# Reordering the first projection of a two-branch encoder block: transposes, bank reads, operand splits and gate outputs

## The chip, the core and the metric

The kernel runs on one core of one Trainium2 chip. The time of a kernel is the device time of one execution in microseconds (us); for each kernel the median of several runs is given. The engines named below are PE (matrix multiply, with its weight loads PEld), DVE (vector), ACT (scalar and activation), POOL (GpSimd) and SP, which here only issues DMAs.

## The reference

One layer (DEPTH is 1) of a block over a sequence of 2048 rows of 1024 float32 values:

```
xn = rmsnorm(x, norm1_g)
z = xn @ w_in                       # [pool | q | f | i | o | branch gates]
gates = sigmoid(zg + b_gate)
ya = pool_mixer(u_pool, ...) @ w_pa
yb = hgrn2_mixer(zq, zf, zi, zo, ...) @ w_pb
x = x + (gates[0] * ya + gates[1] * yb) @ w_o
x = x + conv_glu_ffn(rmsnorm(x, norm2_g), w_up, conv_w, conv_b, w_down)
return rmsnorm(x, final_g)
```

The pooling mixer takes means over windows of 2, 4, 8 and 16 rows. The HGRN2 mixer is a gated linear recurrence with 4 heads of 128; its value input is zi and its output is multiplied by silu(zo). The feed-forward part has 2816 hidden channels for value and gate, with a causal convolution of width 3.

## The kernel before

**Tiling.** The 2048 rows are worked on in two rounds of 1024 rows. A round holds two blocks of 512 rows, b and b+1. Each round runs the input projections, the two mixers, the output projection and the feed-forward part. Weights come in from memory as raw tiles of 128 x 512.

**Seven products.** Every large matrix product splits the rows, the contraction and the columns into halves, and forms the 2 x 2 block product with seven multiplications, called P1 to P7, in place of eight. Each of the seven multiplies one combination of x blocks with one combination of weight blocks. The combinations of x (table FORM) are B11 for P1, B21 for P2, T2 for P6, T1 for P5, T3 for P7, T4 for P4 and B22 for P3. With x12 and x22 the two halves of block b+1, T1 is x12 - B11, T2 is x22 - T1, T3 is B11 - T2, T4 is B21 - T2 and B22 is -x22. Each has four tiles, k = 0 to 3.

**Split operands.** Every operand is split into a high and a low part in the type fp32r: ACT casts the high part, then DVE subtracts it from the source for the low part (function split, lines 615 and 616, for x; Stream.convert, lines 212 and 213, for weights). A product takes three matmuls (high x high, high x low, low x high).

**The first projection.** Function proj_io, line 1187 on, makes zi ("v") and zo ("z") for 1024 rows. It is the first large product of a round. It runs the passes in the order P1, P2, P6, P5, P7, P4, P3. One pass has four weights (k) times four groups of 128 rows (j) times three matmuls, 48 in all. The results stand in PSUM in four tiles per letter: P1 in X, P2 in Y, P6 and P7 and P4 accumulate in Z, P5 and P3 accumulate in V. PSUM has eight such tiles (pool "banks" with bufs=8), so a letter needs four of them and must wait until others have been read. The readers are: e1, a copy of X by ACT (L1210); v, which reads Y after P2 (L1064); u2, which reads Z after P6 (L1214); u3, which reads Z after P7 (L1216) and must have done so before P4 adds to the same Z; z of block b+1, which is u3 + V and must have read V before P3 adds to it; z of block b, which reads Z after P4 (L1063). Both z go through SiLU on ACT and out by a DMA on SP.

**Where the x forms come from.** forms_a_task transposes block b on PE for B11 and B21. forms_b_task does the same for block b+1: turned(k) transposes one 128-column group (four transposes of 128 x 128, L678) into one PSUM tile, and turned(k) and turned(k + 4) together serve T1 and T2 of number k (L766, DVE). T3 and T4 are subtractions of tiles in SBUF (L796 and L804, DVE).

**Weights of this projection.** The weights have numbers in the stream: w0 to w3 for P1, w4 to w7 for P2, w8 to w11 for P6, w12 to w15 for P5, w16 to w19 for P7, w20 to w23 for P4 and w24 to w27 for P3. Those of P6 take two additions on DVE, those of P7 and P3 one (L352); all take the split. Intermediate sums are kept in memory by DMAs on SP and loaded again for P5 and P3.

**What sets the order.** The functions emit instructions in Python order. Tasks (generators) are stepped between matmuls: every six matmuls make a tick, which advances the weight stream by one and steps each task that is due. A planner then orders each engine's instructions by emission and by its own simulation of when each is ready, so the order on the chip is not the emission order. On the chip each engine works its list in order. behind(a, b) forces a after b on one engine without a semaphore; stream.pins does so for a weight's split. In proj_io the first matmul of each k of P2 from k = 1 is put behind the last transpose made so far, the four T4 and B22 tiles are split in turns, and u3 is followed at once by z of block b+1.

Of the kernel before, what the change touches and what calls it, by code (L numbers as in the profile page):

```python
# [15 lines left out]
ALU = mybir.AluOpType  # L16
# [14 lines left out]
NT = TB // P  # L31
# [21 lines left out]
FIRST = ("P1", "P6", "P5")  # L53
# [27 lines left out]
def tile_trunk(  # L81
# [16 lines left out]
    pe, act, dve, pool, sp = nc.tensor, nc.scalar, nc.vector, nc.gpsimd, nc.sync  # L98
# [9 lines left out]
    def slot(name, cols=TB, dt=F32):  # L108
        return slots.tile([P, cols], dt, tag="s", name=name, padded_shape=[P, 528])

    def bank(name, cols=512):
        return banks.tile([P, cols], F32, tag="b", name=name, padded_shape=[P, 512])

    def f32(ap):
        return ap.bitcast(F32)
# [30 lines left out]
    def mm(*args, **kw):  # L146
        count[1] = pe.matmul(*args, **kw)  # L147
        count[0] += 1
        if count[0] % MM_PER_TICK == 0:
            tick()  # L150
# [89 lines left out]
    def behind(ins, other):  # L240

        tc.add_manual_dep(ins.ins, other.ins.name, mybir.DependencyInfo(
            mybir.DependencyClass.NoSync, mybir.DependencyReason.DATA), reason="behind")
# [17 lines left out]
    stream = Stream()  # L261
# [285 lines left out]
    def col(o):  # L547
        return cols[:, o : o + 1]
# [57 lines left out]
    setup = []  # L606


    def split(src, name, on_pool=False):
        hi = slot(name + "h", TB, F32R)  # L610
        lo = slot(name + "l", TB, F32R)
        if on_pool:
            pool.tensor_scalar(hi, src, 1.0, 0.0, ALU.mult, ALU.add)
        else:
            act.copy(hi, src)
        dve.tensor_tensor(lo, src, f32(hi), ALU.subtract)  # L616
        return hi, lo

    def chain_t(ps, w_of, xs, start=True, stop=True):
# [8 lines left out]
    def n_step(ps, w, xk, j, first, last, mark=None, **kw):  # L628
        xh, xl = xk
        a, b = xh[:, j * P : (j + 1) * P], xl[:, j * P : (j + 1) * P]  # L630
        mm(ps, a, w[:, 0], start=first, stop=False, **kw)
        if mark is not None:
            behind(count[1], mark)
        mm(ps, a, w[:, 1], start=False, stop=False, **kw)
        mm(ps, b, w[:, 0], start=False, stop=last, **kw)
# [40 lines left out]
    def transpose(ps, xs, j, k):  # L676
        c = (k % 4) * P
        return pe.transpose(ps[:, j * P : (j + 1) * P], xs[j, k // 4][:, c : c + P], ident)  # L678
# [68 lines left out]
    def forms_b_task(src, gain, forms, full, after, go, early):  # L747
        name = f"{src[0]}{src[1]}_"
        xs = {}
        while early and not forms["B21"]:  # L750
            yield 1
        yield from norm_rows(src, name, xs, after, int(early))
        while not go():
            yield 2
        t1, b12, b22 = [], [], []

        def turned(k):
            ps = bank(f"{name}t{k}")
            for j in range(NT):
                forms["turned"] = transpose(ps, xs, j, k)  # L760
            return ps

        def minus(key, k, ps, x1, c=None, op=ALU.subtract):
            t = slot(f"{name}{key}{k}")
            c = gain + (k if c is None else c)
            dve.scalar_tensor_tensor(t, ps, col(c), x1, ALU.mult, op)  # L766
            return t


        t3 = []  # L770
        for k in range(4):
            while len(full["B11"]) <= k:
                yield 4
            p12 = turned(k)
            p22 = turned(k + 4)
            t = slot(f"{name}b{k}")
            act.activation(t, p22, AF.Copy, scale=negs[:, gain + k + 4 : gain + k + 5])
            b22.append(t)
            t1.append(minus("t1", k, p12, full["B11"][k]))
            t2 = minus("t2", k, p22, t1[k], k + 4)  # L780
            if src[0] == "m":
                t = slot(f"{name}t3{k}")
                pool.tensor_tensor(t, full["B11"][k], t2, ALU.subtract)
                t3.append(t)
            elif not early:
                t3.append(minus("t3", k, p12, b22[k], op=ALU.add))
            forms["T2"].append(split(t2, f"{name}T2{k}"))
            full["T2"].append(t2)
            yield 1
        for k in range(4):  # L790
            forms["T1"].append(split(t1[k], f"{name}T1{k}"))
            yield 5
        for k in range(4):
            if early:
                t = slot(f"{name}t3{k}")
                dve.tensor_tensor(t, full["B11"][k], full["T2"][k], ALU.subtract)  # L796
                t3.append(t)
            forms["T3"].append(split(t3[k], f"{name}T3{k}"))
            yield 1
        for k in range(4):  # L800
            while len(full["B21"]) <= k:
                yield 4
            t4 = slot(f"{name}t4{k}")
            (dve if src[0] == "x" else pool).tensor_tensor(t4, full["B21"][k], full["T2"][k],  # L804
                                                           ALU.subtract)
            forms["T4"].append(split(t4, f"{name}T4{k}"))
            forms["B22"].append(split(b22[k], f"{name}B22{k}"))
            yield 1

# [377 lines left out]
    def proj_io(b0, forms, late, vd, zd):  # L1187
        bk = {}
        e1, u2, u3 = {}, {}, {}

        def temp(d, key, j):
            d[j] = slot(f"io{b0}_{key}_{j}")
            return d[j]

        def out_v(hf, j, a):
            t = slot(f"v{b0}_{hf}_{j}")
            ins = value(t, a, bk["Y" if hf == 0 else "V"][j])
            if not (b0 or hf):
                behind(ins, stream.low)
            sp.dma_start(vd[hf][:, j, :], t)  # L1200

        def out_z(hf, j, a):
            t = slot(f"z{b0}_{hf}_{j}")
            value(t, a, bk["Z" if hf == 0 else "V"][j])
            act.activation(t, t, AF.Silu)
            sp.dma_start(zd[hf][:, j, :], t)

        def after(p, j):
            if p == "P1":
                act.copy(temp(e1, "e1", j), bk["X"][j])  # L1210
            elif p == "P2":
                out_v(0, j, (e1[j], "add"))
            elif p == "P6":
                dve.tensor_tensor(temp(u2, "u2", j), e1[j], bk["Z"][j], ALU.subtract)  # L1214
            elif p == "P7":
                dve.tensor_tensor(temp(u3, "u3", j), bk["Z"][j], e1[j], ALU.subtract)  # L1216
                out_z(1, j, (u3[j], "add"))
            elif p == "P4":
                out_z(0, j, (e1[j], "from"))
            elif p == "P3":  # L1220
                out_v(1, j, (u2[j], "sub"))

        for p in IO_ORDER:
            if p == "P7" and not b0:
                setup.append(Task(setup_task()))
            xs = need(forms, FORM[p], late)
            kb = "Y" if p == "P2" else BANK[p]
            if kb not in bk:
                bk[kb] = [bank(f"io{b0}_{kb}_{j}") for j in range(NT)]
            for k in range(4):  # L1230
                if (p, k) == GO_IO[b0 > 0]:
                    go_io[0] = True
                mark = None
                if p == "P2" and k and not b0:
                    while len(forms["T2"]) < k:
                        late.step()
                    mark = forms["turned"]
                    while len(stream.tiles) < 9 + k:
                        stream.convert()
                w = stream.get("io")  # L1240
                if (p, k, b0) == ("P1", 0, 0):
                    xh, xl = xs[0]
                    for n in range(3):
                        for j in range(NT):
                            mm(bk[kb][j], (xl if n == 2 else xh)[:, j * P : (j + 1) * P],
                               w[:, n % 2], start=n == 0, stop=False, skip_group_check=True)
                    stream.used(1)
                    continue
                for j in range(NT):
                    n_step(bk[kb][j], w, xs[k], j, p in FIRST + ("P2",) and k == 0, k == 3, mark,  # L1250
                           skip_group_check=True)
                    mark = None
                    if k == 3:
                        after(p, j)
                stream.used(1)
# [453 lines left out]
    for b in range(0, SEQ // TB, 2):  # L1709
        forms, task, late = nxt  # L1710
        if b:
            join(task)
        forms, task, late = mixer(b, forms, late)
# [52 lines left out]
```

## Time and profile before

| | us |
|---|---|
| median of 3 runs | 2564.29 |
| lowest and highest run | 2561.81, 2565.13 |
| the profiled execution | 2561.69 |
| its span, first to last instruction | 2560.0 |
| PE busy | 2516.1 (98%) |
| DVE busy | 1979.3 (77%) |
| ACT busy | 1177.7 (46%) |
| POOL busy | 749.1 (29%) |

In the views of the trace, a row of the waits reads "engine, tile, line <- engine, tile, line that it waited for: total us, times, longest". A row of the windows gives, for a stretch of the span, each engine's busy time with its number of instructions, then the clock granted to PE as a share of the full one, the busy share of the DMA engines, and GB/s. A row of the timeline gives start, duration, engine, line, operation, output <- inputs, number of instructions merged, and in brackets the idle time of the engine before it and what ended that.

### The profile page before, as it was taken

Reading aid. Unit: us, or ns where it says so; the run is one execution under the profiler, and the core shown is the slowest. Engines: PE = TensorE matmul, PEld = TensorE weight load, DVE = VectorE, ACT = ScalarE, POOL = GpSimd, SP = SyncE. Lnnn points to the kernel's source line nnn. Section 1 sums busy time; section 2 is a strip of 40 time slices with the busy share of each in tenths; the row PEclk is TensorE's granted clock in tenths of the full one; section 3 lists DMA queues with packets and bytes.
Section 4 is the critical chain, followed back from the end, with each engine's and each line's share of the span. In section 5 each row is a group of like instructions: output and inputs, shape, how many; then the busy total and the mean of one; then the engine's idle time right before and its main releaser. Section 6 shows DMA issues by size and latency. Waiting matters only on the chain.

```text
span 2560.0 us, 35657 instructions
## 1 busy us (share of the span) xinstructions
PE 2516.1 (98%) x11508; PEld 2055.6 (80%) x11508; DVE 1979.3 (77%) x3518; ACT 1177.7 (46%) x2218; POOL 749.1 (29%) x1117
## 2 busy tenths in 40 slices
PE   8899999999999999999999999999999999999998
PEld 7688877888788888888887888888887888888887
DVE  7798879588889787885585777675978987778755
ACT  5434433424645454554454344442355554545534
POOL 1244344001544334461230111200034433334410
PEclk9999999999999999999999999999999999999999
DMA  6777768768788878997344343446442454446952
GB/s 235 247 191 210 225 181 244 240 206 244 196 241 247 220 230 239 257 356 261 129 153 149 94 134 118 128 150 229 144 165 94 153 152 144 145 139 229 333 162 99
DMA packets 252332, 493.76 MB, mean 193 GB/s; under 512 B 26544, under 2 KB 43056, under 8 KB 251824
## 3 DMA queue, kind: packets, MB, share of 16 engines
q1 hardware_dynamic: 185664, 315.70, 38.2%
q0 software_dynamic: 41504, 110.64, 16.8%
q10 hardware_dynamic: 24976, 65.13, 7.3%
q8 instruction: 91, 1.49, 0.2%
q14 instruction: 97, 0.79, 0.1%
HBM read 381.79 MB, written 187.17 MB: 222 GB/s over the span
## 4 chain that ended last, share of the span: by engine, by line
PE 71%; DVE 1%; ACT 1%; issue 0%; POOL 0%; POOLq 0%; DVEq 0%; ACTq 0%
PE dn_P L147 16%; PE up_Z L147 14%; PE up_V L147 9%; PE up_X L147 9%; PE wo_P L147 3%; PE gr_Z L147 3%; PE gr_X L147 2%; PE gr_V L147 2%; PE pb L147 2%; PE pa L147 2%; PE fr_Z L147 1%; PE io_Z L147 1%; PE io_V L147 1%; PE fr_X L147 1%; PE fr_V L147 1%; PE pl L931 1%
## 5 line engine op out<-in xcount | busy, mean ns | idle before, releaser
L212 ACT CAST ops<-raw 128x512 fp32r<-128x512 f32 x736 | 454.5, 620 | 839.3 <-PE dn_P L147 175.6
L213 DVE TENSOR_TENSOR ops<-raw,ops 128x512 fp32r<-128x512 f32 x736 | 547.9, 748 | 210.0 <-ACT ops L212 204.7
L1502 DVE SCALAR_TENSOR_TENSOR e<-h,cols,e 128x512 f32<-128x512 f32 x176 | 143.6, 818 | 30.8 <-ACT e L1500 24.0
L1500 ACT ACTIVATE e<-h,cols 128x512 f32<-128x512 f32 x176 | 142.6, 814 | 24.8 <-DVE h L1064 18.4
L1505 DVE SCALAR_TENSOR_TENSOR e<-h,cols,e 128x512 f32<-128x512 f32 x176 | 133.8, 769 | 2.8
L866 POOL DMA_DIRECT2D g_P<-dg_P x154 | 84.4, 555 | 161.9 <-PE dn_P L147 113.2
L1171 POOL TENSOR_TENSOR gf_P<-e,e 128x512 f32<-128x512 f32 x44 | 60.8, 1384 | 149.5 <-DVE e L1511 96.0
L1297 POOL TENSOR_TENSOR q<-q,qs 128x512 f32<-128x512 f32 x16 | 21.9, 1366 | 201.5 <-ACT qs L1296 194.4
L1171 POOL TENSOR_TENSOR gf_P<-gf_P,e 128x512 f32<-128x512 f32 x44 | 59.2, 1345 | 71.9 <-DVE e L1511 71.4
L1495 POOL COPY h<-h 128x2 f32<-128x2 f32 x88 | 40.4, 471 | 113.9 <-DVE h L1063 107.0
L1509 ACT ACTIVATE e<-e 128x512 f32<-128x512 f32 x88 | 55.5, 631 | 38.5 <-DVE e L1505 38.2
L1497 POOL COPY hist<-h 128x2 f32<-128x2 f32 x88 | 35.8, 407 | 118.2 <-DVE h L1064 116.4
L1064 DVE TENSOR_TENSOR h<-up_u,up_V 128x512 f32<-128x512 f32 x88 | 60.1, 683 | 13.3 <-PE up_V L147 12.8
L1334 ACT ACTIVATE gt<-gt,cols 128x512 f32<-128x512 f32 x48 | 34.8, 725 | 73.9 <-DVE gt L1064 55.0
L1146 DVE TENSOR_TENSOR x<-x,wo_P 128x512 f32<-128x512 f32 x88 | 55.9, 678 | 12.2 <-PE wo_P L147 12.0
L1146 DVE TENSOR_TENSOR ac<-ac,dn_P 128x512 f32<-128x512 f32 x72 | 47.0, 680 | 16.6 <-PE dn_P L147 16.4
L1525 POOL DMA_DIRECT2D dg_P<-gf_P x88 | 50.6, 575 | 7.9 <-POOL gf_P L1171 7.2
L1098 ACT COPY up_e<-up_X 128x512 f32<-128x512 f32 x44 | 25.8, 587 | 58.0 <-PE up_X L147 50.7
L916 POOL COPY qm<-q 128x64 f32<-128x64 f32 x64 | 21.1, 347 | 105.1 <-DVE q L922 36.9
L931 PE MATMUL pl<-qm,k 128*128 128x192 f32 x256 | 50.3, 326 | 0.3 <-DVE qm L920 0.3
L1495 POOL COPY h<-hist 128x2 f32<-128x2 f32 x88 | 46.3, 534 | 7.7 <-DVE m_T42l L616 7.7
L931 PEld LDWEIGHTS pl<-qm,k 128*128 128x128 f32 x256 | 44.2, 189 | 5.0 <-issue 0.6
(1301 smaller groups left out, 8107.4 us busy)
## 6 DMA issues: line engine op xcount, KB each, us to landing
g_P<-dg_P POOLq DMA_DIRECT2D x154, 256.0 KB, 6.0
raw<-in_w_up_t SPq DMA_DIRECT2D x132, 256.0 KB, 3.1
raw<-in_w_in_t SPq DMA_DIRECT2D x98, 256.0 KB, 3.3
dg_P<-gf_P POOLq DMA_DIRECT2D x88, 256.0 KB, 3.9
dg_P<-e SPq DMA_DIRECT2D x66, 256.0 KB, 3.3
raw<-in_w_dn SPq DMA_DIRECT2D x66, 256.0 KB, 3.6
x<-in_x SPq DMA_DIRECT2D x64, 256.0 KB, 5.1
gd<-gt ACTq DMA_DIRECT2D x64, 256.0 KB, 3.3
```

What stands on the lines that cost most here:

```text
L147: count[1] = pe.matmul(*args, **kw)
L212: self.mark = act.copy(hi, v)
L213: low = self.low = dve.tensor_tensor(lo, v, f32(hi), ALU.subtract)
L866: eng.dma_start(t, d)
L931: ins = pe.matmul(pa_[:, c * 192 : c * 192 + 192], ks[:, (i + c) * P : (i + c + 1) * P], mv[:, c].rearrange("p s x -> p (s x)"), start=Tru ...
L1064: return dve.tensor_tensor(dst, t, ps, ALU.add if how == "add" else ALU.subtract)
L1146: dve.tensor_tensor(t, t, ps[j], ALU.add if sg > 0 else ALU.subtract)
L1171: pin(eng.tensor_tensor(t, x0, x1, op))
L1495: pool.tensor_copy(h[:, 0:2], hist[:, mt] if hf == 0 else hs[s, 0][:, TB : TB + 2])
L1500: in_turn(act.activation(t, h[:, 2:], AF.Identity, bias=col(o_cb + mt), scale=col(o_cw + 4 * MF + mt)))
L1502: in_turn(second(dve.scalar_tensor_tensor(t, h[:, 1 : 1 + TB], col(o_cw + 2 * MF + mt), t, ALU.mult, ALU.add)))
L1505: dve.scalar_tensor_tensor(t, h[:, 0:TB], col(o_cw + mt), t, ALU.mult, ALU.add)
```

## The change

All of it concerns the first projection of the first round (the flag early, or b0 equal to 0); the second round keeps the old order.

1. Transposes for T2 in the second pass. Before P2's k = 1 the code now emits T1 and T2 of two numbers instead of one, before k = 2 of three, before k = 3 of all four. The list forms["turned"] holds the last transpose of every turned group. The matmuls of k = 1 for j = 2 and 3 are put behind the transposes of T2 number 0, all four j of k = 2 behind those of number 1, and all four j of k = 3 behind the first group of number 2. Before, only the j = 0 matmul of each k was bound. The weights w9 to w11 are emitted one k earlier.
2. Bank reads ahead of the last two T4 tiles. T4 numbers 2 and 3 are emitted only when all four u3 have been, and their subtraction is put behind the last u3 on DVE.
3. B22 behind T4. The four B22 splits are emitted after all four T4 splits, not in turns with them.
4. The gate behind T4. z of block b+1 (addition, SiLU, store) is emitted before k = 2 of P4, not right after each u3.
5. T4's weights behind T3. The split of w20 is put behind the split of T3's last tile on ACT and DVE.

```diff
+            up = act.copy(hi, src)
+        low = dve.tensor_tensor(lo, src, f32(hi), ALU.subtract)
+        last_split[0] = up, low
...
             for j in range(NT):
-                forms["turned"] = transpose(ps, xs, j, k)
+                ins = transpose(ps, xs, j, k)
+            forms.setdefault("turned", []).append(ins)
...
             forms["T3"].append(split(t3[k], f"{name}T3{k}"))
+            if early:
+                stream.pins[20] = last_split[0]
...
+            while early and k > 1 and len(forms.get("u3", ())) < 4:
+                yield 1
+            ins = (dve if src[0] == "x" else pool).tensor_tensor(t4, full["B21"][k],
+                                                                 full["T2"][k], ALU.subtract)
+            if early and k > 1:
+                behind(ins, forms["u3"][3])
             forms["T4"].append(split(t4, f"{name}T4{k}"))
+            if not early:
+                forms["B22"].append(split(b22[k], f"{name}B22{k}"))
+            yield 1
+        while len(forms["B22"]) < 4:
+            k = len(forms["B22"])
             forms["B22"].append(split(b22[k], f"{name}B22{k}"))
             yield 1
...
-                dve.tensor_tensor(temp(u3, "u3", j), bk["Z"][j], e1[j], ALU.subtract)
-                out_z(1, j, (u3[j], "add"))
+                ins = dve.tensor_tensor(temp(u3, "u3", j), bk["Z"][j], e1[j], ALU.subtract)
+                forms.setdefault("u3", []).append(ins)
+                if b0:
+                    out_z(1, j, (u3[j], "add"))
...
-                if p == "P2" and k and not b0:
-                    while len(forms["T2"]) < k:
-                        late.step()
-                    mark = forms["turned"]
-                    while len(stream.tiles) < 9 + k:
+                if p == "P2" and not b0:
+                    if k:
+                        while len(forms["T2"]) < min(k + 1, 4):
+                            late.step()
+                        mark = forms["turned"][k + (k > 1)]
+                    while len(stream.tiles) < min(10 + k, 12):
                         stream.convert()
+                if (p, k, b0) == ("P4", 2, 0):
+                    for j in range(NT):
+                        out_z(1, j, (u3[j], "add"))
...
-                    n_step(bk[kb][j], w, xs[k], j, p in FIRST + ("P2",) and k == 0, k == 3, mark,
-                           skip_group_check=True)
-                    mark = None
+                    n_step(bk[kb][j], w, xs[k], j, p in FIRST + ("P2",) and k == 0, k == 3,
+                           mark if k > 1 or j > 1 else None, skip_group_check=True)
```

No arithmetic instruction, transpose or DMA is added or removed; they change places.

More of the change, by code (lines that the diff above doesn't have):

```diff
@@ L606, in tile_trunk @@
     setup = []
+    last_split = [None]
     def split(src, name, on_pool=False):
@@ L612, in split @@
         if on_pool:
-            pool.tensor_scalar(hi, src, 1.0, 0.0, ALU.mult, ALU.add)
+            up = pool.tensor_scalar(hi, src, 1.0, 0.0, ALU.mult, ALU.add)
         else:
-            act.copy(hi, src)
-        dve.tensor_tensor(lo, src, f32(hi), ALU.subtract)
+            up = act.copy(hi, src)
+        low = dve.tensor_tensor(lo, src, f32(hi), ALU.subtract)
+        last_split[0] = up, low
         return hi, lo
@@ L803, in forms_b_task @@
             t4 = slot(f"{name}t4{k}")
-            (dve if src[0] == "x" else pool).tensor_tensor(t4, full["B21"][k], full["T2"][k],
-                                                           ALU.subtract)
-            forms["T4"].append(split(t4, f"{name}T4{k}"))
+            while early and k > 1 and len(forms.get("u3", ())) < 4:
[4 more added lines that the diff above has]
+                behind(ins, forms["u3"][3])
+            forms["T4"].append(split(t4, f"{name}T4{k}"))
+            if not early:
[3 more added lines that the diff above has]
+            k = len(forms["B22"])
             forms["B22"].append(split(b22[k], f"{name}B22{k}"))
```

## The prediction

> **What bounds the kernel now.** I read the page's totals first, then the list of PE's waits, then the windows of the passes that the change touches, and last the timelines of PE, DVE, ACT, POOL and SP inside them.
>
> ```profile
> span 2560.0 us, 35657 instructions
> ## 1 busy us (share of the span) xinstructions
> PE 2516.1 (98%) x11508; PEld 2055.6 (80%) x11508; DVE 1979.3 (77%) x3518; ACT 1177.7 (46%) x2218; POOL 749.1 (29%) x1117
> ```
>
> PE is busy in all but 43.9 us of the span (2560.0 - 2516.1). A reordering can win only those, and whatever PE spends at a reduced clock. PE's waits, longest first:
>
> ```profile
> PE io_Z L147 <- DVE io_u L1216: 8.4, 1, 8.4
> PE pl L971 <- DVE q L890: 5.2, 3, 2.3
> ...
> PE io_Z L147 <- DVE x_t L766: 1.9, 2, 1.1
> ...
> PE x_t L678 <- DVE x_t L766: 1.3, 2, 1.1
> ...
> PE io_Z L147 <- ACT x_T32h L615: 1.1, 1, 1.1
> ```
>
> Four of these rows (8.4, 1.9, 1.3 and 1.1) lie in the first projection. The passes follow, cut at PE's own starts: P2 with P6, P5, P7, the hole before P4, P4, P3.
>
> ```profile
> 27.50:57.35 29.85, 26.64 (x130) 21.09 (x129) 23.36 (x39) 13.67 (x27) 1.79 (x5) 1.00 0.46 151
> 57.35:68.45 11.10, 11.10 (x49) 8.83 (x48) 9.37 (x17) 3.93 (x7) 0.00 (x0) 1.00 0.98 324
> 68.45:81.43 12.98, 11.88 (x49) 8.79 (x48) 11.40 (x19) 5.61 (x10) 1.58 (x3) 1.00 0.80 269
> 81.43:89.83 8.40, 0.00 (x1) 0.04 (x1) 6.32 (x12) 3.41 (x6) 3.81 (x10) 0.64 0.00 0
> 89.83:102.91 13.08, 13.08 (x49) 10.55 (x49) 11.66 (x24) 7.98 (x12) 2.96 (x12) 0.84 0.66 205
> 102.91:114.02 11.11, 11.11 (x50) 9.01 (x49) 9.99 (x11) 3.65 (x6) 7.86 (x8) 1.00 0.80 294
> ```
>
> P5 and P3 show what an undisturbed pass takes, 11.1 us. Against that: P2 with P6 idles 29.85 - 26.64 = 3.2, P7 idles 12.98 - 11.88 = 1.1, the hole is 8.4, and P4 is 13.08 - 11.1 = 2.0 longer, at a granted clock of 0.84 after 0.64 in the hole. That makes 14.7 us, the most that the change can win inside these passes. DVE is busy in 72.1 of the 86.5 us, so it paces the stretch, and the change frees none of its time: it only sorts its list.
>
> **The change part by part.** One DVE operation on 128x512 costs 0.61 to 0.69 us in the rows below, which I use throughout.
>
> *T2's transposes (P2, P6).*
>
> ```profile
> 35.61 1.25 PE L678 MATMUL x_t<-ident,x_xs 128*128 128x128 f32 x10
> ...
> 48.98 0.73 PE L147 MATMUL io_Z<-ops,x_T20h 128*128 128x512 f32 x2 [1.12 <-DVE x_t L766]
> ```
>
> ```profile
> 30.97 0.88 DVE L672 TENSOR_SCALAR x_xs<-x,x_3r 128x512 f32<-128x512 f32 x2
> ...
> 36.68 0.75 DVE L766 SCALAR_TENSOR_TENSOR x_t<-x_t,cols,x_b 128x512 f32<-128x512 f32 x1 [2.79 <-PE x_t L678]
> ...
> 53.83 0.69 DVE L213 TENSOR_TENSOR ops<-w11s,ops 128x512 fp32r<-128x512 f32 x1 [0.74 <-ACT ops L212]
> ```
>
> The rows of x are scaled by 31.85 (30.97 + 0.88), but the transposes stand at 35.61 behind P2 matmuls in PE's list, while DVE idles 2.79 us for them. Later PE pays that back, waiting for T1/T2 to leave PSUM. With half of k = 1 and all of k = 2 bound behind the transposes, they can run at about 32, after the k = 0 products and two of k = 1. DVE then starts T1 some 4 us sooner, and w11's split (53.83) comes near 49.5. PE's own work allows 27.5 + 26.6 = 54.1 for the end of P6, with w11 wanted a k-pass of 2.8 us (11.1 / 4) before it, at 51.3. So DVE is no longer last. But letter Z still needs T2 number 3 off PSUM, so I leave 0.7 of the 3.2: **-2.5**. Bounds: -3.2, and +1.0 if the 32 transposes, now mandatory points in PE's list, catch a tile not yet free (the two such waits now are 1.3 together). DVE's additions for w9 to w11 move one k earlier; at worst one stands ahead of a T1, which is 0.6 us and inside the 0.7.
>
> *P5.* It starts sooner by the same amount. Its window shows DMA share 0.98, and w12 to w15 and T1 must come sooner too; they follow w11 on DVE and move with it. I cost this at nothing; if the loads don't move, the 2.5 is given back here.
>
> *T4's weights behind T3 (P7).*
>
> ```profile
> 74.11 1.89 DVE L213 TENSOR_TENSOR ops<-raw,ops 128x512 fp32r<-128x512 f32 x3
> 75.91 0.68 DVE L616 TENSOR_TENSOR x_T32l<-x_t,x_T32h 128x512 fp32r<-128x512 f32 x1
> ...
> 77.88 0.69 DVE L616 TENSOR_TENSOR x_T33l<-x_t,x_T33h 128x512 fp32r<-128x512 f32 x1
> 78.49 0.69 DVE L804 TENSOR_TENSOR x_t<-x_b,x_t 128x512 f32<-128x512 f32 x1
> ...
> 88.39 0.68 DVE L616 TENSOR_TENSOR x_B223l<-x_b,x_B223h 128x512 fp32r<-128x512 f32 x1
> 89.00 0.68 DVE L1216 TENSOR_TENSOR io_u<-io_Z,io_e 128x512 f32<-128x512 f32 x1
> ```
>
> Three splits for T4's weights (1.89 us, with three casts on ACT) stand ahead of T3 number 2, for which PE waits 1.1. Only w20 is pinned; w21 and w22 take later ops buffers and I take them to follow it. **-1.1**, between -1.1 and 0. Behind the pin on DVE's list stand w20's split and P4; the raw buffers that w20 to w23 release feed P3's weights, wanted some 11 us later, and a raw tile lands in 3.3 us, by the page's list of loads:
>
> ```profile
> raw<-in_w_in_t SPq DMA_DIRECT2D x98, 256.0 KB, 3.3
> ```
>
> *The hole.* Call P7's end E. The first u3 could read Z at about E - 2, but DVE has from 78.49 to 89.07 the whole T4 and B22 chain ahead of it: four subtractions and eight splits, 12 x 0.65 = 7.8, a mask cast, and four gaps of 0.68 in which ACT casts. Now only T4 numbers 0 and 1 come ahead. T3's last split ends at 78.57, E - 2.9; without the three weight splits (1.9) at about E - 4.2. From there DVE has the two subtractions, two T4 splits and two weight splits, 6 x 0.61 = 3.7, to E - 0.5, then the first u3 to E + 0.1. PE started 0.15 after it (89.68 to 89.83), and I allow one more operation ahead: P4 starts at **E + 0.7**, not E + 8.4, which is **-7.7**. Bounds: -8.4, and -4 if four more weight or B22 splits (2.5 us) and ACT gaps get ahead. T4 numbers 2 and 3 follow the last u3 (E + 2.6): two subtractions, an ACT cast, two splits, done by E + 5.8; P4 wants them 5.6 and 8.3 us after its start, so at E + 6.3 and E + 9.0.
>
> *The clock.* The only PE wait here with a reduced clock is the 8.4; the 1.1 in P7 has 1.00. With 0.7 left, P4 takes 11.1: **-2.0**, or 0 if some 4 us of wait stay. [...]
>
> *B22 and the gate behind T4 (P3).* What left the hole must now fit into P4's 11.1 us: three u3 and two T4 tiles (3 + 4 operations), two weight splits, four B22 splits, four z, two of P3's four weights (sum and split each): 7 + 2 + 4 + 4 + 4 = 21 operations, 21 x 0.61 = 12.8 us against the 11.8 from E to P4's end. The last z is not wanted at P3's first matmul but 2 us later, so a wait of **+0.5** (0 to +3). The other two weights (4 operations) are wanted 5.6 us into P3. The four z stores move behind P4 loads on SP; ACT's SiLUs and their table load move with them, and ACT has over 3 us free in each window. POOL's mask building is not moved.
>
> *Behind the projection.*
>
> ```profile
> 103.02 1.84 POOL L411 TENSOR_TENSOR w29s<-raw,raw 128x512 f32<-128x512 f32 x1 [5.87 <-DMA raw<-in_w_in_t]
> ```
>
> ```profile
> 116.80 0.39 PE L147 MATMUL fr_Z<-x_T20h,ops 128*128 128x512 f32 x1
> ```
>
> The next unit's summed weight waits for its raw tiles, which SP issues after P3's sums. Those sums come no later against P3 than now, so the 13.8 us from the sum to its use cover it. The planner lays out everything behind anew:
>
> ```profile
> 120.00:1400.00 1280.00, 1266.80 (x5795) 1034.38 (x5795) 1003.20 (x1729) 588.19 (x1109) 440.47 (x597) 1.00 0.75 222
> 1400.00:2560.00 1160.00, 1147.21 (x5246) 939.02 (x5244) 883.84 (x1635) 527.69 (x990) 280.20 (x444) 0.99 0.48 156
> ```
>
> PE idles 13.2 + 12.8 = 26.0 us there. I put **+0.5** on a new layout, between -2 and +3.
>
> The sum is -2.5 - 1.1 - 7.7 - 2.0 + 0.5 + 0.5 = **-12.3 us**. The profiled execution took 2561.69 (span 2560.0 and 1.69 around it), so 2549.4 by its own measure. It was the fastest execution shown, 2.6 below the median 2564.29; from the median the sum gives **2552.0 us**, my forecast.
>
> **The rivals.**
>
> *The hole shrinks, the rest doesn't.* DVE paces the stretch, and the two early parts only move its list. If the planner fills DVE's early gap with weight sums, P6 and P7 keep their 4.3, and if more than one split stays ahead of u3 the remainder is 3 and P3 waits 1. [...] For it speaks DVE's 72.1 of 86.5 us; against it the 2.79 that DVE spends waiting for PE's transposes.
>
> *It doesn't do what it says.* w21 and w22 get ahead of w20, and w20 to w23, three B22 splits and T4's casts still stand before u3 in DVE's list; the remainder is over 4 and the clock still falls: 4 from the hole, less 1 for P3, within the measurement: 2561.3. Against it: u3 is bound ahead of T4's subtractions by an explicit dependency, and B22 is emitted after them.
>
> *Slower: the layout behind it.* The level products of the recurrence (pl) sit in PE's list at places the planner chose, and three of them wait 5.2 us for q, 1.7 each. If the new layout puts them ahead of their q more often, each costs 1.7. The gain up to there, 12.8, is used up by 8 such waits (13.6), which is where this decides; 11 of them, 18.7, end at 2564.29 - 12.8 + 18.7 = 2570.2. For it: a few us of input timing change every later choice. Against it: only three among the rounds' many levels wait so now, and PE is at 99% in both windows.
>
> **How the numbers follow.** Runs here differ by 3.3 us (2561.81 to 2565.13); 0.2%, 5.1 us, is about what a measurement tells from no change. Chances: my forecast (a gain over 7) 0.57, the hole alone 0.18, no effect 0.10, slower through the layout 0.15. The hole alone counts as faster. So faster 0.75, same 0.11, slower 0.14 (part of the layout case ends within the bound). The best sum, all of 14.7 and 2 from the layout, would be 2547.6 from the median; runs near the lower end take another 1.5. The upper end takes in the hole alone with its worse bounds and a part of no effect: 2546 to 2562.5. The likeliest case alone spans 2547 to 2557.
>
> **What would show it.** After the change: the first T2 transposes near 32, DVE's wait of 2.79 gone, P6 ending near 54.6; no wait on T3; the row for io_Z on io_u under 2 us or gone, a granted clock of 1.00 through P4; P3 beginning by E + 12.5; the next unit's first matmul near 114.0 - 12.8 = 101.2. It is wrong if a wait over 4 us stands anywhere between 27 and 101, if DVE's T1 still starts after 35, or if PE's idle time past the projection grows by more than 3.

## The result and the profile after

| | before | changed |
|---|---|---|
| median, us (6 runs each) | 2565.09 | 2553.57 |
| lowest and highest | 2561.81, 2566.67 | 2551.22, 2555.53 |
| the profiled execution | 2561.69 | 2554.45 |
| its span | 2560.0 | 2552.7 |

The changed kernel takes 0.9956 of the time before, 95% interval 0.9943 to 0.9969: 11.5 us less by the medians. The prediction said 2552.0, 12.3 less. The two profiled executions lie 7.2 us apart, since that of before was the fastest of its six runs and that of after the second slowest.

Busy times hardly move: PE is busy for 2518.6 us in place of 2516.1, DVE for 1978.0 in place of 1979.3, ACT for 1176.0 in place of 1177.7.

The passes of the changed kernel, cut at the same places as before (P2 with P6, P5, P7, the hole, P4, P3; the columns are the stretch, its length, each engine's busy time and instructions, PE's granted clock, DMA share, GB/s):

```profile
27.08:52.92 25.84, 25.84 (x129) 21.42 (x128) 23.64 (x40) 14.62 (x29) 1.82 (x5) 1.00 0.55 180
52.92:63.98 11.06, 11.06 (x50) 9.02 (x48) 9.44 (x17) 2.86 (x5) 0.00 (x0) 1.00 0.96 320
63.98:75.22 11.24, 11.24 (x49) 8.83 (x47) 9.65 (x16) 4.99 (x9) 5.29 (x12) 1.00 0.66 227
75.22:78.31 3.09, 0.00 (x0) 0.03 (x1) 2.41 (x5) 0.62 (x1) 0.00 (x0) 0.85 0.83 266
78.31:92.20 13.89, 13.89 (x48) 11.18 (x49) 12.97 (x27) 7.76 (x13) 2.73 (x10) 0.79 0.39 127
92.20:104.45 12.25, 12.25 (x54) 9.94 (x53) 10.93 (x17) 6.33 (x12) 9.45 (x11) 1.00 0.99 329
```

P2 with P6 went from 29.85 to 25.84, P7 from 12.98 to 11.24, the hole from 8.40 to 3.09. P4 became longer, 13.08 to 13.89, at a clock of 0.79. P3 has 12.25 because the planner put four matmuls of the next unit into it (at 98.71 to 99.40; the count of 54 also takes in matmuls that cross the window's edges).

For comparing runs I use one number, "passes": from P2's first matmul to the end of P3's last, less 0.23 us for each of the next unit's matmuls in between. It is 86.5 before and 76.2 after, 10.2 less before rounding.

Five rows of DVE's timeline tell why a hole of 3.09 is left:

```profile
71.13 0.76 DVE L618 TENSOR_TENSOR x_T33l<-x_t,x_T33h 128x512 fp32r<-128x512 f32 x1 [0.74 <-ACT x_T33h L617]
71.81 0.72 DVE L812 TENSOR_TENSOR x_t<-x_b,x_t 128x512 f32<-128x512 f32 x1
72.46 2.53 DVE L213 TENSOR_TENSOR ops<-raw,ops 128x512 fp32r<-128x512 f32 x4
...
76.87 0.69 DVE L618 TENSOR_TENSOR x_T41l<-x_t,x_T41h 128x512 fp32r<-128x512 f32 x1 [0.68 <-ACT x_T41h L617]
77.48 2.48 DVE L1231 TENSOR_TENSOR io_u<-io_Z,io_e 128x512 f32<-128x512 f32 x4
```

All four weight splits of P4 (2.53 us) stand between T3's last split and u3, and T4 number 1 is subtracted only after T4 number 0's split, so that its cast on ACT leaves another gap of 0.68. The first u3 starts at 77.48, 2.3 us after P7's end.

### The profile page after: what moved, and what is told of

It is laid out like the page before. It is cut to its first block, busy times and chain, and to the rows that moved or that the text cites. A ratio compares the mean times of both kernels' runs of the same rounds, so it can differ in the third digit from the quotient of the medians.

```text
span 2552.7 us, 35665 instructions
## 1 busy us (share of the span) xinstructions
PE 2518.6 (99%) x11508; PEld 2058.3 (81%) x11508; DVE 1978.0 (77%) x3518; ACT 1176.0 (46%) x2218; POOL 753.4 (30%) x1117
## 4 chain that ended last, share of the span: by engine, by line
PE 71%; DVE 1%; ACT 1%; issue 0%; POOL 0%; POOLq 0%; DVEq 0%; ACTq 0%
PE dn_P L147 16%; PE up_Z L147 14%; PE up_V L147 9%; PE up_X L147 9%; PE wo_P L147 3%; PE gr_Z L147 3%; PE gr_X L147 2%; PE pb L147 2%; PE gr_V L147 2%; PE pa L147 2%; PE fr_Z L147 1%; PE io_Z L147 1%; PE fr_X L147 1%; PE io_V L147 1%; PE fr_V L147 1%; PE pl L946 1%
## 5 line engine op out<-in xcount | busy, mean ns | idle before, releaser
L1161 DVE TENSOR_TENSOR x<-x,wo_P 128x512 f32<-128x512 f32 x88 | 56.0, 681 | 12.2 <-PE wo_P L147 12.0
```

Of the source, the lines that this page charges most:

```text
L1161: dve.tensor_tensor(t, t, ps[j], ALU.add if sg > 0 else ALU.subtract)
```

## The experiments

Theories at the start: **the parts add**, each part of the change taking away its own wait, against **DVE paces the stretch**, so that what one part saves grows back at the next wait. The times are medians; the ratio is to runs of the kernel before on the same chip, with its 95% interval, and is what to compare across chips. Hole, P4 and passes are from each run's trace.

| run | median, us | ratio | hole | P4 | passes |
|---|---|---|---|---|---|
| before | 2565.09 | | 8.4 | 13.1 | 86.5 |
| changed | 2553.57 | 0.9956 (0.9943 to 0.9969) | 3.1 | 13.9 | 76.2 |
| t2_alone | 2559.30 | 0.9980 (0.9971 to 0.9989) | 8.4 | 13.7 | 82.3 |
| no_t2 | 2557.06 | 0.9974 (0.9963 to 0.9985) | 3.3 | 12.8 | 80.0 |
| no_pin | 2552.07 | 0.9954 (0.9942 to 0.9967) | 2.1 | 12.7 | 75.0 |
| gate_back | 2553.85 | 0.9968 (0.9957 to 0.9980) | 2.9 | 12.8 | 75.0 |
| b22_turns | 2552.57 | 0.9961 (0.9949 to 0.9974) | 4.6 | 12.7 | 76.6 |
| u3_late | 2558.85 | 0.9984 (0.9975 to 0.9992) | 8.4 | 12.7 | 80.4 |
| after_again | 2553.41 | 0.9961 (0.9948 to 0.9975) | 3.1 | 13.9 | 76.1 |
| hold22 | 2550.81 | 0.9956 (0.9943 to 0.9968) | 2.2 | 12.7 | 74.6 |
| hold21_subs | 2548.59 | 0.9941 (0.9927 to 0.9955) | 0.7 | 11.2 | 73.7 |
| hold21_again | 2549.28 | 0.9948 (0.9935 to 0.9960) | 0.3 | 11.2 | 73.5 |
| hold21_subs_z | 2550.44 | 0.9957 (0.9945 to 0.9970) | 0.7 | 11.8 | 74.5 |
| hold21_z2 | 2551.47 | 0.9960 (0.9948 to 0.9973) | 0.7 | 11.2 | 75.4 |

**t2_alone** is the kernel before with the transposes' part:

```diff
-                    while len(forms["T2"]) < k:
+                    while len(forms["T2"]) < min(k + 1, 4):
                         late.step()
-                    mark = forms["turned"]
+                    mark = forms["turned"][k + (k > 1)]
...
-                    while len(stream.tiles) < 9 + k:
+                    while len(stream.tiles) < min(10 + k, 12):
```

> The kernel before with part 1 of the change alone (T2's transposes in the second pass). Theory 'the parts add': DVE's first T1 moves from 36.7 to about 33.3, P6 ends 4 us sooner against P2's start, the hole before P4 stays near 8.4 us since DVE's chain moves as a whole, and the time is 4 us under the kernel before (about 2561). Rival 'the hole eats it': P4 starts where it did, near 89.5, the hole grows to about 12, and the time is that of the kernel before (2565, within 1.5).

P2 with P6 took 25.83, the hole stayed 8.4 and P4 started at 84.91, not at 89.5:

```profile
84.91 1.19 PE L147 MATMUL io_Z<-ops,x_T40h 128*128 128x512 f32 x2 [8.41 <-DVE io_u L1217]
```

The passes fell by 4.1 and the time by 0.0020 of 2564.1, 5.1 us. The parts add: the wait before P4 isn't fed by what P2 and P6 save, because DVE's chain moves along with PE.

**no_t2** is the changed kernel with the same lines put back.

> The changed kernel with part 1 undone. 'The parts add': PE's waits for T1 and T2 are back (3.2 us), the hole stays near 3.1, and the time is 4 us over the changed kernel (2557.5). 'The hole eats it': P4 starts where it does in the changed kernel, near 78.3, with no hole left, and the time is that of the changed kernel (2553.5, within 1.5).

P2 with P6 took 29.84 again, the hole 3.3, and the passes 80.0, 3.8 above the changed kernel. The other parts alone save 0.0026, 6.7 us; with t2_alone's 5.1 that makes 11.8, against 11.5 measured for the whole.

**no_pin** takes two lines out of the changed kernel:

```diff
-            if early:
-                stream.pins[20] = last_split[0]
```

> The changed kernel without the pin of T4's weights behind T3. As predicted, the pin is worth the wait on T3: P7 gets 1.1 to 1.7 us longer, the hole stays 3.1, and the time is 1 to 2 us over the changed kernel. Rival 'the pin only moves the four weight splits from before T3 into the hole': P7 is longer by 1.1 to 1.7, the hole shorter by as much, P4 starts within 0.4 of where it did; the time is then the same, or up to 2.8 us shorter if PE's clock stays at 1.00 through the shorter hole.

The rival held. P7 is 1.0 longer (12.2), with a wait on T3 of 0.7, and the hole is 1.0 shorter (2.1). By these two PE stops together the pin is worth nothing. The passes are even 1.2 shorter without it, all of it in P4: there PE's clock was halved for 3.4 us (79.05 to 82.46), in the changed kernel for 6.8 (77.40 to 84.23).

**gate_back** emits z of block b+1 right after each u3 again:

```diff
-                if b0:
-                    out_z(1, j, (u3[j], "add"))
+                out_z(1, j, (u3[j], "add"))
...
-                if (p, k, b0) == ("P4", 2, 0):
-                    for j in range(NT):
-                        out_z(1, j, (u3[j], "add"))
```

> The changed kernel with part 4 undone: each z of block b+1 again right after its u3. The four additions then stand among the u3, so the last u3 and T4 numbers 2 and 3 come 2.4 us later on DVE. If those have slack (T4 number 2 is done 4.7 us before PE uses it in the changed kernel): the hole stays near 3.1 and the time is that of the changed kernel within 1.5, which makes part 4 worth nothing by itself. If the gate's place matters: P4 waits inside and the time is 2 us or more over the changed kernel.

The hole is 2.9 and no new wait stands in P4. By the trace the gate's move is worth nothing by itself. The time doesn't settle it: the ratio, 0.9968, is 3 us above the changed kernel's, with overlapping intervals.

**b22_turns** splits B22 in turns with T4 again (`if not early` becomes `if True`).

> The changed kernel with part 3 undone: B22's splits in turns with T4's. Two B22 splits stand ahead of u3; one fills the gap in which ACT casts (0.7), the other adds itself: hole 3.7 to 4.4 in place of 3.1, P4 begins 0.6 to 1.3 later, and the time is about 1 us over the changed kernel. Rival 'B22's place made the hole': the hole is over 5 and the time 3 us or more over it.

The hole grew to 4.6, a little more than expected, yet the passes only to 76.6, as P4 took 12.7, not 13.9. B22's place is worth 1.5 us of hole; of that the passes show 0.4, and the ratio, 0.9961, is 1.3 us above the changed kernel's, inside its interval.

**u3_late** drops the rule that T4 numbers 2 and 3 follow u3:

```diff
-            while early and k > 1 and len(forms.get("u3", ())) < 4:
-                yield 1
...
-            if early and k > 1:
-                behind(ins, forms["u3"][3])
```

> The changed kernel with part 2 undone: T4 numbers 2 and 3 may come ahead of u3 again, everything else as changed. By the sum over DVE's list, two subtractions, two splits and two gaps for ACT (4 x 0.61 + 2 x 0.7 = 3.8), and the two B22 splits that come with them, make the hole about 7 to 8.4, and the time is 3 to 5 us over the changed kernel. If the other parts carry the gain without part 2: the hole stays under 4 and the time within 1.5 of it.

The hole is back to 8.4, with two B22 splits in it as expected, and the passes are 4.2 over the changed kernel. This rule carries the gain at the hole: 5.3 us.

**hold21_subs** tests what fills the remaining hole. The stream stops at w21 until u3 has been emitted, and T4's first two subtractions stand side by side:

```diff
+                if j >= self.hold:
+                    return
...
+            if early and k == 0:
+                t4s = [slot(f"{name}t4{i}") for i in range(2)]
+                for i in range(2):
+                    dve.tensor_tensor(t4s[i], full["B21"][i], full["T2"][i], ALU.subtract)
...
+            if p == "P7" and not b0:
+                stream.hold = 21
+            if p == "P4" and not b0:
+                stream.hold = 1 << 30
+                for n in range(21, 24):
+                    stream.pins[n] = last_split[0][0], forms["u3"][3]
```

> The changed kernel, with the splits of w21 to w23 held behind u3 and the first two T4 subtractions side by side, so that one weight split and two T4 tiles stand ahead of u3 on DVE. If the four weight splits and the gap for ACT's cast make the hole of 3.1 us: the hole is under 1, PE's clock stays 1.00 in P4, and the time is about 5 us under the changed kernel (2548.5). If the hole is the chain from T3 to T4 itself: it stays over 2 and the time within 1.5 of the changed kernel. If the held weights come late: PE waits for ops inside P4, by 1 to 3 us.

The first reading held: the time is 2548.59, by the ratios 3.8 us under the changed kernel. PE's waits from P2 to P3 are then these two, the upper one new, of P3 on its first weight:

```profile
PE io_V L147 <- DVE ops L214: 1.4, 1, 1.4
PE io_Z L147 <- DVE io_u L1241: 0.7, 1, 0.7
```

**hold22** holds only w22 and w23 (22 for 21 above) and leaves the subtractions one behind the other. So two weight splits stand ahead of u3, as the prediction had assumed.

> The changed kernel with w22 and w23 held behind u3, so that two weight splits stand ahead of it as the prediction assumed, not four; the T4 subtractions stay one behind the other. Two splits less are 2 x 0.61 = 1.2: a hole of 1.8 to 1.9. If the splits are not what fills it: 3.1 as before. Whether PE's clock falls after 1.9 us is open: it did after 2.1 (run no_pin) and not after 0.7.

The hole is 2.2, a little over the 1.8 to 1.9. From the start of T3's last split to the first u3, DVE takes 5.19 us (72.24 to 77.43) where the changed kernel takes 6.35 (71.13 to 77.48), which is the 1.2 expected for two splits. But PE ended P7 only 3.85 us after that start, not 4.09, and so waits 0.24 longer. T4 number 1's split still waits 0.74 for its cast:

```profile
72.24 0.75 DVE L621 TENSOR_TENSOR x_T33l<-x_t,x_T33h 128x512 fp32r<-128x512 f32 x1 [0.74 <-ACT x_T33h L620]
...
76.82 0.69 DVE L621 TENSOR_TENSOR x_T41l<-x_t,x_T41h 128x512 fp32r<-128x512 f32 x1 [0.74 <-ACT x_T41h L620]
77.43 2.48 DVE L1234 TENSOR_TENSOR io_u<-io_Z,io_e 128x512 f32<-128x512 f32 x4
```

In hold21_subs the same stretch of DVE takes 3.62:

```profile
71.59 0.69 DVE L621 TENSOR_TENSOR x_T33l<-x_t,x_T33h 128x512 fp32r<-128x512 f32 x1 [0.74 <-ACT x_T33h L620]
...
75.21 2.48 DVE L1241 TENSOR_TENSOR io_u<-io_Z,io_e 128x512 f32<-128x512 f32 x4
```

So two weight splits make 0.9 of the 3.1. The third split and the gap, gone together in hold21_subs, take another 1.6 us out of DVE's list and 1.5 to 1.9 out of the hole; they weren't tried apart.

**after_again** and **hold21_again** are the changed kernel and hold21_subs once more, unaltered, on one chip with hold22.

> The changed kernel again, unaltered, to stand beside the next runs on one chip. Its passes from P2 to P3 take the 76.2 us of the first trace within 1.5; the difference, if any, is PE's clock after the hole of 3.1 us, which may fall at another moment.

> The kernel of run hold21_subs again beside the changed kernel: hole 0.7, clock 1.00 through P4, passes 73.7 us, and 2 to 5 us under the changed kernel.

Both gave their traces again (passes 76.1 and 73.5), and hold21_again took 4.1 us less than after_again. hold21_subs is the faster version that the experiments point to; the intervals of its ratios still overlap those of the changed kernel, its passes don't.

**hold21_subs_z** and **hold21_z2** went for P3's wait of 1.4. The first puts z behind w24's split, the second B22 numbers 1 to 3 behind z. Both also emit w24 ahead of the gate (not shown):

```diff
+            if hf and not b0:
+                behind(ins, stream.lows[24])
```

```diff
+            while early and k and not forms.get("gate"):
+                yield 1
```

> The kernel of run hold21_subs, with the four z of block b+1 behind the split of P3's first weight w24 on DVE. There P3 waits 1.4 us for that split, which stands behind z and two weight sums. If that is the whole wait: it falls under 0.7 and the time is 1 us under hold21_subs (2547.6). If the z then hold P3 up in its place (P3 may not write V before they have read it): the wait stays, under another name, and so does the time.

> The kernel of run hold21_subs with B22 numbers 1 to 3 behind the gate's additions on DVE, so that P3's first weight and z come sooner. If P3's wait of 1.4 us is only the order of DVE's list: the wait goes, the passes take about 72.5 us and the time is 1 to 1.5 us under hold21_again, hardly more than can be told. If DVE's work as such is the limit now: a wait as long stands somewhere else in P3 or behind it.

Neither won. In the first, PE's wait came back under three names: 1.2 for the next unit's weight (ops, ACT), 0.7 for a weight of P3 (ops, DVE) and 0.5 for z.

In the second, the planner put w25's and w26's sums and two B22 splits ahead of w24's split, the wait was 1.8, and the clock behind it was 0.50 (92 to 94).

## Why the prediction came out

**T2's transposes (-2.5, bounds -3.2 and +1.0): right in kind, too small.** They ran at 31.25 (said: about 32), w11's split at 48.85 (said: near 49.5), and no wait was left. P2 with P6 gave 4.0, beyond my bound of 3.2, since I took PE's busy 26.64 as its own work. Of it 0.8 went too: the changed kernel has the same matmuls in 25.84. Why those 0.8 stood there as busy time isn't shown.

```profile
31.25 1.91 PE L681 MATMUL x_t<-ident,x_xs 128*128 128x128 f32 x16
```

**P5 (0): right**, 11.06.

**T4's weights behind T3 (-1.1): the wait went, the gain didn't.** P7 lost 1.7, of which no_pin gives the pin 1.0 (the rest comes with part 1: P7 takes 12.2 in t2_alone); but the four splits that the pin moved came to stand in the hole, 1.0 us of PE's time (no_pin against changed). The step failed where I let only two of them go ahead of u3.

**The hole (-7.7): mis-sized; it gave -5.3.** The mechanism, u3 ahead of the second half of T4, is what carries it (u3_late). The steps that failed are the list that the sum put on DVE between T3's last split and u3, and the place of that split. The sum had two weight splits and no gap, 3.7 us; the trace has four weight splits and a gap of 0.68, 5.7 us (71.81 to 77.48). The sum ended T3's last split at E - 4.2; its own figures (2.9, with 1.9 of splits gone before it and E 1.1 sooner) give E - 3.7, and the trace has E - 3.4. These are 2.0 and 0.8 us, of which the allowance of one more operation took up 0.4. So the remainder is 3.1, not 0.7. The list that the sum assumed was not run: hold22 has its two weight splits, but keeps the gap (2.2); the hold21 runs have no gap, but only one weight split (0.7 and 0.3). With one split of 0.6 more these would give about 0.9 to 1.3, an estimate.

**The clock (-2.0): wrong.** P4 didn't get 2.0 shorter but 0.8 longer, outside the bound of 0. The step that failed is the limit: the prediction let the 2.0 be lost only if some 4 us of wait stay, a limit that no run shows; here the clock fell to 0.50 in a wait of 3.1 us (at 77.40), and as well after 2.1 in no_pin and 2.2 in hold22 (0.50 from 80 to 83). The trace of before already held a fall of the clock without a wait that long (below). In hold21_subs and hold21_again, with 1.00 throughout, P4 takes 11.2, against the 11.1 that I had put down.

**B22 and the gate (+0.5): at its lower bound.** P3 has no wait, so the term is 0. B22's place is worth 1.5 us of hole (b22_turns), the gate's nothing by its trace (gate_back).

**Behind the projection (+0.5): open.** From the end of the next unit's T2 stage to the end of the span, the same matmuls took 3.4 us longer in the profiled execution of the changed kernel, but 0.4 longer in after_again (before, changed, after_again):

```profile
119.59:2560.00 2440.41, 2414.41 (x11041) 1973.76 (x11039) 1887.20 (x3364) 1116.10 (x2099) 720.67 (x1041) 1.00 0.62 191
108.94:2552.70 2443.76, 2417.30 (x11041) 1975.15 (x11039) 1888.73 (x3364) 1115.60 (x2099) 723.60 (x1041) 1.00 0.63 191
109.54:2550.33 2440.79, 2414.07 (x11041) 1972.35 (x11039) 1888.64 (x3364) 1115.54 (x2099) 719.89 (x1041) 1.00 0.62 191
```

PE's idle time there grew by 0.5 and 0.7, so the layout did not add the 3 us of idle time that would have refuted the forecast. Inside the stretch the changed kernel had two falls of the clock of 3.4 us each (at 210 and 395) that after_again did not have; this fits the 3.0 between these two. It doesn't explain the 3.4 against before, which lost as long to one fall (1408 to 1415). By the medians the whole gain is 11.5, with 8.0 to 14.6 by the interval; the passes and P2's earlier start (0.4) make 10.6 of it. That shows no loss behind the projection, and leaves room for one of 2.6.

The rivals: "the hole shrinks, the rest doesn't" falls with t2_alone, though the remainder of 3 that it named did come; "it doesn't do what it says" was half there, as w20 to w23 did stand before u3; the slower layout didn't come (the waits of pl on q are 5.2 in three, as before). That my sum of -12.3 came near the 11.5 is in part luck: the T2 stage and P7 gave 2.1 more, and the hole and the clock 5.2 less, than their terms, and P3 and the rest took 2.3 less than allowed. The mechanisms of the transposes and of u3 held, the limit put down for the clock did not. Of the signs that the prediction named, the early transposes, the end of DVE's wait and of the wait on T3, and P6's end came (52.9, said 54.6). The row of io_Z on io_u (3.1, not under 2), the clock in P4 (0.79, not 1.00) and the start of P3 (E + 17.0, not E + 12.5) did not.

## What to carry to other kernels

When an instruction list is reordered, write out the new list of the pacing engine to the last operation: a pin that takes four operations out of one wait puts them into the next. Free a buffer's reader (u3) before preparing operands that are needed only later, and let two-engine chains (subtract, cast, split) run two at a time so that the second hides the first's gap. Compare traces by stage lengths, because one execution's span here carries a few us of clock luck: 3.0 between two executions of the changed kernel, behind the projection alone.

## What the hardware showed

**After the same wait PE's clock was halved in one execution and not in the next.** The changed kernel waits 2.29 us for q at the same place in two profiled executions. In the first the 16 small matmuls behind it took 3.24 us, in after_again 2.02:

```profile
394.26 3.24 PE L986 MATMUL pl<-q,k 128*128 128x128 f32 x16 [2.29 <-DVE q L905]
```

```profile
393.74 2.02 PE L986 MATMUL pl<-q,k 128*128 128x128 f32 x16 [2.29 <-DVE q L905]
```

The windows just behind, first and second execution:

```profile
394.00:398.00 4.00, 3.74 (x18) 3.67 (x19) 4.00 (x11) 2.10 (x5) 1.54 (x2) 0.60 0.94 207
```

```profile
394.00:398.00 4.00, 4.00 (x27) 3.55 (x27) 4.00 (x10) 1.89 (x4) 2.18 (x3) 1.00 0.86 190
```

By the granted clock in narrow windows, the first execution had 0.50 from 394.84 to 398.25, for 3.41 us, and from 77.40, in the hole, to 84.23, for 6.83 us. The wait for q lay at 391.97 to 394.26 in the first execution and at 391.45 to 393.74 in after_again. Why one of them was followed by 0.50 and the other by 1.00 isn't shown: no run moved a wait to test it.

In the kernel before, half the clock came within a wait of 1.65 us (0.59 from 1408 to 1409), with another of 1.22 shortly ahead of it:

```profile
1406.22 1.13 PE L971 MATMUL pl<-q,k 128*128 128x128 f32 x8 [1.22 <-DVE q L890]
1409.00 0.79 PE L147 MATMUL gr_X<-x_f4h,ops 128*128 128x512 f32 x1 [1.65 <-ACT gr_e L1098]
```

```profile
1409.00:1414.00 5.00, 5.00 (x12) 3.94 (x13) 4.86 (x14) 0.42 (x1) 1.24 (x3) 0.50 0.18 54
```

With holes of 2.1, 2.2, 2.9, 3.1, 3.3, 4.6 and 8.4 us the clock fell, and with 0.3 and 0.7 it did not; P4 then took 12.7 to 13.9, against 11.2 in hold21_subs, so by an estimate from these one fall cost 1.5 to 2.7 us. The waits of 2.2 us in hold22's hole and of 2.29 us for q in the changed kernel were each followed by a clock of 0.50. How much idle time it takes isn't shown.

**ACT and DVE in turns cost a gap of 0.7.** The chains of subtraction (DVE), cast (ACT) and split (DVE) shown here leave DVE idle for 0.68 to 0.74 us where no other work stands between them in its list; in the hole that gap is as long as one DVE operation (0.61). In hold21_again, with two such chains side by side, the two T4 splits start at 73.26 and 73.86, with no idle time before either.
